# Windowed attention beside sliced projections, modulation steps two at a time, and a gapped convolution

## The chip, the cores and the metric

The kernel runs on one core of a Trainium2 chip. The metric is device time in microseconds (us) of one execution, lower is better, quoted as a median of several runs.

## The reference

The model has two layers. It carries 512 latent tokens and 256 context tokens of width 1024, 768 tokens in all. A conditioning vector makes nine modulation vectors per layer (shift, scale and gate for three sublayers) by one product with `w_mod`; context tokens have their own. Cut to what matters, for the latent tokens of a layer:

```python
m = silu(c) @ w_mod[l] + b_mod[l]                       # 9 vectors of 1024
h += 0.5 * m[2] * swiglu(modulate(rms_norm(h, g1), m[0], m[1]), ...)
z = split_in(modulate(rms_norm(h, gm), m[3], m[4]) @ w_in[l])
o_a = dense_attend(mla_q(z[0]), mla_kv(z[1], z[2]))     # 4 heads, 768 keys
o_b = b_g * dw_conv(c_g * x, w_sc)                      # 3 taps
o_c = window_attend(q, k, v, k_ctx, v_ctx, sink)        # blocks of 128, neighbours and context
o_d = silu(layer_norm(dw_conv(a * sigmoid(g), w_cf) + b))   # 31 taps
h += m[5] * concat(o_a, o_b, o_c, o_d) @ w_out[l]
h += 0.5 * m[8] * swiglu(modulate(rms_norm(h, g2), m[6], m[7]), ...)
```

In layer 0 the context tokens take the same way. In layer 1 they only give keys and values, so there 512 tokens are queries. The latent stream is normed once more at the end.

## The kernel before

Activations lie with channels on partitions and tokens along the free axis. Each large product is done in fp32r with both sides split into a high and a low part: `mm3` (L162) issues three matmuls, low by high, high by low, high by high. The split of a weight is a copy on ACT (L133) and a subtraction on VectorE (L134). Each layer runs the FFN, the mixer, the output projection (`out_proj`) and the second FFN, which in layer 1 only sees the latent tokens.

The modulation vectors are made beside all of this. `mod_group` (L179) computes four blocks of 256 columns in eight steps. A step loads 512 KB of `w_mod` on SP's queue into one of two buffers (`mraw`) and issues four matmuls of 32 rows by 256 columns into one PSUM bank (`pmod`). `fill()` takes one step; it is called after units of work in the FFNs and in the mixer, so that these steps lie between other matmuls. `need()` takes all steps that are still missing when a vector is wanted.

`mixer` runs four groups. All read one product with `w_in`, cut into 17 tiles of 128 columns, each a sum over eight blocks of 128 channels in PSUM (`proj_parts`). In the order of the program these are first the four conformer tiles (CFA, CFG); then the conformer convolution on VectorE, put at the lowest priority (`P_CONV`), so that its taps are placed behind whatever else VectorE can do; then the tiles of MLA's keys and values (KV) and queries (QA, QB), each with its sums of squares; then five of the windowed attention (WQ, WK, WV) and six of the short convolution (SC). The first MLA queries are made inside the last of these. A pool of three PSUM tiles of two banks serves the projections; the third is given back afterwards and becomes two single banks for transposes.

Then a loop runs over units. A `Latent` unit handles one head and two blocks of 128 queries of MLA against 768 keys (12 units in layer 0, 8 in layer 1). A `Window` unit handles one block of queries for the two heads that share keys (12 and 8). Each unit goes through softmax (scores on TensorE, reduce L818 or L870 on VectorE, exp on ACT, scaling on GpSimd or VectorE), `turned` (transposes L595 and splits) one step of the loop later, and `values` (L765, L766) two steps later. All latents come first, then the windows; one `fill()` stands after each step. The windows' operands are made two steps before the latents end, the conformer norm during and after the windows, and `out(i)` splits a finished block of 128 mixed channels for `out_proj`.

The program's text is not the final order of each engine: a scheduler places instructions by readiness and priority, and `rise` raises or lowers the priority of what is inside it.

The convolution takes 31 taps of one operation each per segment: latent (512) and context (256) tokens apart in layer 0, so that no tap reads across the seam.

## Time and profile before

| | us |
|---|---|
| median of 3 runs | 2715.44 (2715.19 to 2719.1) |
| the profiled execution | 2716.3 |
| its span | 2714.5 |
| TensorE busy in it | 2640.3 (97%) |
| VectorE busy | 2014.1 (74%) |
| ACT busy | 1116.9 (41%) |

The mixer of layer 0 lies between about 585 and 904 us of the span, that of layer 1 between about 2050 and 2308. The FFNs, with the modulation steps between their matmuls, fill most of the rest. A row of the timeline has the start, the length, engine, line, operation, output and inputs; neighbours of one kind are one row with their number (x6), and a bracket tells how long the engine had stood idle and for whom. PEclk is the clock granted to TensorE as a share of full speed.

### The profile page before, as it was taken

The page shows a single profiled execution, that of the slowest core. Times are in us where ns is not written, and L with a number is a line of the kernel's source. Part 1 is how long each engine was busy: PE and PEld are TensorE (multiplying, and loading weights), DVE is VectorE, ACT ScalarE, POOL GpSimd, SP SyncE. Part 2 cuts the span into 40 slices and gives each one's busy share as a digit, 9 for nine tenths or more (in the row PEclk, how much of TensorE's full clock was granted, in tenths as well). Part 3 has the DMA queues.
Part 4 walks back from the last instruction along what each step waited for, and adds up shares of the span by engine and source line. Part 5 has one row for each costly group of instructions (what it writes and reads, how often), then busy time and mean ns, then how long its engine had stood idle before and what let it go on. Part 6 is the DMA issues. An engine that isn't in the chain of part 4 may idle for free.

```text
span 2714.5 us, 40707 instructions
## 1 busy us (share of the span) xinstructions
PE 2640.3 (97%) x16021; PEld 2443.1 (90%) x16021; DVE 2014.1 (74%) x3940; ACT 1116.9 (41%) x2098; POOL 66.0 (2%) x88
## 2 busy tenths in 40 slices
PE   7999999999988999999999999999999989999998
PEld 5999999988866989999999999999998866899998
DVE  5777667679787476777667867776678786788887
ACT  4324323343376442333234523343244376544444
POOL 0000000000022000000000000000000022000000
PEclk9999999999989999999999999999999989999999
DMA  7323223321123342323223132222223223323322
GB/s 269 109 91 104 86 87 101 101 85 56 53 80 128 95 139 82 107 88 107 80 86 124 49 100 69 64 78 63 63 79 101 69 67 113 117 86 104 99 94 78
DMA packets 78271, 254.67 MB, mean 94 GB/s; under 512 B 8704, under 2 KB 14336, under 8 KB 77824
## 3 DMA queue, kind: packets, MB, share of 16 engines
q1 hardware_dynamic: 78080, 252.08, 29.2%
q8 instruction: 125, 2.05, 0.3%
q14 instruction: 66, 0.54, 0.1%
HBM read 249.95 MB, written 2.10 MB: 93 GB/s over the span
## 4 chain that ended last, share of the span: by engine, by line
PE 91%; DVE 4%; ACT 3%; DMA 1%; issue 1%; POOL 0%; DVEq 0%; SPq 0%; ACTq 0%; POOLq 0%
PE ps L162 74%; PE pone L162 8%; PE pmod L162 3%; PE pmod L179 3%; PE ps L595 1%; DMA mraw<-in_w_mod 1%; PE pone L765 1%; PE pone L766 1%; ACT f L826 1%; DMA raw<-in_w_gu 0%; ACT f L133 0%; DVE r L134 0%; ACT f L873 0%; POOL f L833 0%; PE pone L272 0%
## 5 line engine op out<-in xcount | busy, mean ns | idle before, releaser
L162 PE MATMUL ps<-x,wh 128*128 128x384 f32 (+1 forms) x3064 | 749.5, 329 | 0.0
L162 PEld LDWEIGHTS ps<-x,wh 128*128 128x128 f32 x3064 | 543.1, 188 | 0.2
L162 PE MATMUL ps<-x,wl 128*128 128x384 f32 (+1 forms) x1532 | 506.5, 331 | 0.0
L133 ACT ACTIVATE wh<-raw 128x512 fp32r<-128x512 f32 x439 | 274.8, 627 | 464.6 <-PE ps L162 313.9
L162 PE MATMUL ps<-t,wh 128*128 128x384 f32 (+2 forms) x1488 | 385.2, 341 | 0.1
L134 DVE TENSOR_TENSOR wl<-raw,wh 128x512 fp32r<-128x512 f32 x439 | 301.6, 688 | 104.9 <-ACT wh L133 102.5
L162 PE MATMUL ps<-r,wh 128*128 128x512 f32 (+3 forms) x1362 | 338.0, 350 | 0.3 <-DVE r L291 0.3
L296 DVE SCALAR_TENSOR_TENSOR h<-ps,hg,h 128x256 f32<-128x256 f32 (+3 forms) x404 | 186.9, 506 | 186.1 <-PE ps L162 185.3
L162 PEld LDWEIGHTS ps<-x,wl 128*128 128x128 f32 x1532 | 287.8, 188 | 12.9 <-issue 10.7
L162 PEld LDWEIGHTS ps<-t,wh 128*128 128x128 f32 x1488 | 269.2, 188 | 7.0 <-DVE t L134 0.4
L133 ACT ACTIVATE wh<-t 128x512 fp32r<-128x512 f32 x217 | 136.3, 630 | 335.9 <-PE ps L162 199.7
L162 PEld LDWEIGHTS ps<-r,wh 128*128 128x128 f32 (+1 forms) x1362 | 228.0, 188 | 31.8 <-DVE r L291 1.5
L450 DVE TENSOR_TENSOR t<-t,ps 128x384 f32<-128x384 f32 (+1 forms) x422 | 217.4, 521 | 51.6 <-PE ps L162 49.9
L162 PE MATMUL ps<-t,wl 128*128 128x384 f32 (+2 forms) x744 | 253.4, 342 | 1.2 <-ACT t L133 1.2
L134 DVE TENSOR_TENSOR wl<-t,wh 128x512 fp32r<-128x512 f32 x217 | 149.3, 690 | 95.2 <-ACT wh L133 94.9
L133 ACT ACTIVATE t<-t 128x384 fp32r<-128x384 f32 (+2 forms) x247 | 130.3, 537 | 213.1 <-DVE t L444 101.9
L162 PE MATMUL ps<-r,wl 128*128 128x512 f32 (+4 forms) x681 | 212.2, 352 | 1.3 <-ACT r L290 1.3
L162 PE MATMUL ps<-x,t 128*128 128x384 f32 (+1 forms) x1308 | 204.4, 310 | 0.0
L162 PEld LDWEIGHTS ps<-x,t 128*128 128x128 f32 x1308 | 194.4, 188 | 0.0
L162 PE MATMUL ps<-t,t 128*128 128x384 f32 (+2 forms) x948 | 188.8, 345 | 0.0
L162 PEld LDWEIGHTS ps<-t,t 128*128 128x128 f32 x948 | 165.4, 188 | 10.9 <-issue 1.2
L134 DVE TENSOR_TENSOR t<-t,t 128x384 fp32r<-128x384 f32 (+2 forms) x247 | 137.7, 569 | 26.0 <-ACT t L133 25.7
(229 smaller groups left out, 3774.1 us busy)
## 6 DMA issues: line engine op xcount, KB each, us to landing
raw<-in_w_gu SPq DMA_DIRECT2D x160, 512.0 KB, 3.8
mraw<-in_w_mod SPq DMA_DIRECT2D x128, 512.0 KB, 4.0
raw<-in_w_dn SPq DMA_DIRECT2D x88, 512.0 KB, 3.7
raw<-in_w_in SPq DMA_DIRECT2D x34, 512.0 KB, 3.5
raw<-in_w_out SPq DMA_DIRECT2D x20, 512.0 KB, 3.5
i<-in_w_mod SPq DMA_DIRECT2D x32, 256.0 KB, 5.9
raw<-in_w_gu SPq DMA_DIRECT2D x32, 256.0 KB, 3.5
h<-in_h SPq DMA_DIRECT2D x4, 768.0 KB, 6.8
```

The costliest lines, as they stand in the source:

```text
L133: self.nc.scalar.activation(hi, x, AF.Copy)
L134: self.nc.vector.tensor_tensor(out=lo, in0=x, in1=hi.bitcast(F32), op=ALU.subtract)
L162: self.nc.tensor.matmul(ps[:, c:e], a, b[:, c:e], start=start and i == 0, stop=stop and i == 2)
L179: nc.tensor.matmul(ps[32 * j:32 * j + 32, :256], self.sc[:, k, :], r[:, j * 256:(j + 1) * 256], start=k == 0, stop=k == KD - 1)
L296: nc.vector.scalar_tensor_tensor(out=self.h[:, k, s:e], in0=ps[:, s - a:e - a], scalar=gate[:, k, i:i + 1], in1=self.h[:, k, s:e], op0=ALU ...
L450: eng.tensor_tensor(out=out, in0=p, in1=q, op=op)
L595: self.nc.tensor.transpose(out, in_, self.ident)
L765: nc.tensor.matmul(po[:, :256], v, p[1], start=start, stop=False)
L766: nc.tensor.matmul(po[:, :256], v, p[0], start=False, stop=stop)
L826: nc.scalar.activation(pr[:, c0:], pss[g][:, c0:TOK], AF.Exp, scale=scale, bias=mx[:, g:g + 1], accum_out=sm[:, g:g + 1])
```

## The change

Order of the mixer. After the conformer tiles only WQ, WK and WV are projected. The window operands follow, and then the loop runs the window units first and the latents after them. The other nine tiles (SC, KV, QA, QB) become a generator, `others`, which yields after each of a tile's eight blocks: 72 pieces, dealt out over the three slots of each window unit. A piece accumulates its 512 columns in `pmod` and the remaining 256 in the last bank of a four-bank PSUM tile (`quad`), whose other banks hold the unit's scores for two heads. No modulation step can run in that time, since `pmod` is taken; an open group is finished first. With the first latent unit all MLA preparation comes at once: query and key weights, rotary parts, queries, keys and values. The conformer norm and the splits `out(i)` move into the latents.

Modulation. `spot()` notes that a step is due and takes both as soon as two are due; it replaces `fill()` in the FFNs and in `out_proj`. In the mixer each step of the loop over latents takes two.

Convolution. The input lies in one row with gaps of 15 zeros before, between and after the segments (written by GpSimd), so a tap is one operation over 783 elements in layer 0 and 512 in layer 1. The norm copies its result back to contiguous tiles.

Buffers. Four wide tiles come in, full tiles go from 14 to 11 and rounded ones from 27 to 26.

```diff
-    WIN, CN = 2, (2, 4, 0, 1)
+    CN = (4, 6, 8, 9)
...
+    GAP = CF_K // 2
+    WIDE = TOK + 3 * GAP
...
+    def spot(self, n=1):
+
+        self.owed += n
+        if self.owed > 1:
+            self.fill(self.owed)
+            self.owed = 0
...
-            self.fill(fills)
+            self.spot(fills)
...
+    def gap_conv(self, y, u, w, bias, n):
+
+        nc = self.nc
+        mid = CF_K // 2
+        for j in [mid] + [j for j in range(CF_K) if j != mid]:
+            if j == mid:
+                nc.vector.tensor_scalar(out=y[:, :n], in0=u[:, j:j + n], scalar1=w[:, j:j + 1], scalar2=bias, op0=ALU.mult, op1=ALU.add)
+            else:
+                nc.vector.scalar_tensor_tensor(out=y[:, :n], in0=u[:, j:j + n], scalar=w[:, j:j + 1], in1=y[:, :n], op0=ALU.mult, op1=ALU.add)
...
-        dbls = self.psum(st, 2, 1024)
-        third = st.enter_context(ExitStack())
-        self.dbl = dbls + self.psum(third, 1, 1024)
-        sgl = deque()
+
+        quad, third = self.psum(st, 1, 2048)[0], self.psum(st, 1, 1024)[0]
+        dbls = deque((quad[:, :1024], quad[:, 1024:]))
+        self.dbl = dbls + deque([third])
+        sgl = deque((third[:, :512], third[:, 512:]))
+        spare = quad[:, 1536:]
...
+        gap = self.GAP
+
+        places = [(a, b, a + i * gap) for i, (a, b) in enumerate(segs)]
         for i in range(2):
+            u = self.wide.popleft()
+            for c in [0] + [p + gap + b - a for a, b, p in places]:
+                nc.gpsimd.memset(u[:, c:c + gap], 0.0)
...
-            u = self.S()
-            nc.scalar.activation(u[:, :n], pg[:, :n], AF.Sigmoid)
-            nc.vector.tensor_tensor(out=u[:, :n], in0=pa[:, :n], in1=u[:, :n], op=ALU.mult)
+            for a, b, p in places:
+                v = u[:, p + gap:p + gap + b - a]
+                nc.scalar.activation(v, pg[:, a:b], AF.Sigmoid)
+                nc.vector.tensor_tensor(out=v, in0=pa[:, a:b], in1=v, op=ALU.mult)
...
+                for g, c, cc in ((0, w.c0[0], SEQ), (1, 1024, TOK)):
+                    q = wqs[kv][g]
...
+                    def near():
...
+                                nc.tensor.matmul(quad[:, c:c + w.n], a, b[:, kc], start=i == 0, stop=False)
...
+                    if g == 0:
+                        near()
+                    for i, (a, b) in enumerate(parts):
+                        nc.tensor.matmul(quad[:, cc:cc + CTX], a, b[:, SEQ:], start=i == 0, stop=i == 1)
+                    if g == 1:
+                        near()
+                wide = w.n + CTX
+                src = [quad[:, c:c + wide] for c in w.c0]
...
-                    ps = self.turn(dbls)
...
-                    nc.vector.reduce_max(mx[:, g:g + 1], ps[:, c0:TOK], axis=AX.X, negate=True)
-                    pss.append(ps)
+                    nc.vector.reduce_max(mx[:, g:g + 1], src[g], axis=AX.X, negate=True)
...
-        for i in range(2):
-            pc = proj(T_SC + 2 + i, n)
-            t = self.S()
...
-            px = proj(T_SC + 4 + i, n)
-            nc.vector.tensor_tensor(out=t[:, :n], in0=px[:, :n], in1=t[:, :n], op=ALU.mult)
...
-            if i == 1:
-                first_queries()
-            pb = proj(T_SC + i, n)
...
+        def slow(t, nt, m=P):
+
+            rw = self.load(win[l, t], 1024)
+            w = [self.unit(rw[:, :512]), self.unit(rw[:, 512:])]
+            pieces = [(0, SEQ, self.mod_ps)] + ([(SEQ, nt, spare)] if nt > SEQ else [])
+            for k in range(KD):
+                wh, wl = w[k // 4]
+                c = slice((k % 4) * P, (k % 4) * P + m)
+                for a, b, ps in pieces:
+                    self.mm3(ps[:m, :b - a], (wh[:, c], wl[:, c]), (x[k][0][:, a:b], x[k][1][:, a:b]), k == 0, k == KD - 1)
+                yield
+            return pieces
+
+        def others():
+
+            for i in range(2):
+                t = self.S()
+                for a, b, ps in (yield from slow(T_SC + 2 + i, n)):
+                    nc.scalar.activation(t[:, a:b], ps[:, :b - a], AF.Copy)
+                for a, b, ps in (yield from slow(T_SC + 4 + i, n)):
+                    nc.vector.tensor_tensor(out=t[:, a:b], in0=ps[:, :b - a], in1=t[:, a:b], op=ALU.mult)
...
+                self.give(t)
+                for a, b, ps in (yield from slow(T_SC + i, n)):
+                    nc.vector.tensor_tensor(out=cv[:, a:b], in0=ps[:, :b - a], in1=cv[:, a:b], op=ALU.mult)
+                ob.append(cv)
...
+            pk = yield from slow(T_KV, TOK)
+            ckv, sq = self.S(), self.S()
...
+            pq = yield from slow(T_QA, n)
...
+            pq = yield from slow(T_QB, TOK, 96)
...
+            mqb = lat["qb"] = self.R()
...
+        units = [Window(t, kv) for kv in range(2) for t in range(nq)]
+        units += [Latent(h, tp) for h in range(4) for tp in range(nq // 2)]
+        nw, per = 2 * nq, nq // 2
+        window_operands()
+        while self.open:
+            self.fill()
...
-        kw = kv_weights()
-        mla_keys(0, kw)
-        self.give(qb)
-        mla_values(kw)
-        units[0].softmax()
-        qw = query_weights()
-        out(2, ob[0])
-        out(3, ob[1])
         lt, lv = self.LAGS
-        cn = conformer_norm()
...
+        cn, rest, done, total = conformer_norm(), others(), 0, 9 * KD
...
+            nonlocal done
+            while done < min(total, round(total * share)):
+                next(rest, None)
+                done += 1
...
+            j = i - nw
+            if j == 0:
+                more(1)
+                for _ in rest:
+                    pass
+                qw, kw = query_weights(), kv_weights()
+                mla_rotary(*qw)
+                mla_queries(0, *qw)
+                mla_keys(0, kw)
+                self.give(lat["kr"])
+                mla_values(kw)
...
                     units[i].softmax()
+            if j in (nq - nw, 0):
+                self.give(*wqs[j == 0], *wks[j == 0])
...
+                if j < 0:
+                    more((3 * i + u + 1) / (3 * nw))
...
-            if i == nl - self.WIN:
-                window_operands()
-            if i - nl in self.CN[:2] or i - len(units) in self.CN[2:]:
...
+            if j in self.CN:
...
+            if j == 5:
                 out(4, oc[0])
-            self.fill()
+                out(5, oc[1])
+            if j == 6:
+                out(2, ob[0])
+                out(3, ob[1])
+            if j == nw // 2 + lv:
+                out(0, oa[0])
+            if j >= 0:
+                self.spot(2)
...
+        out(1, oa[1])
+        self.give(*vt)
...
-            self.fill()
+            self.spot()
...
-    N_R, N_F = 27, 14
+    N_R, N_F, N_WIDE = 26, 11, 4
```

What this does to TensorE's queue is seen at three places. The first is the FFN of layer 0. `ps` are its sums, `x` and `t` activations, `wl` and `wh` split weights, and `pmod<-mraw` a modulation step of four matmuls. Before:

```order
L162 MATMUL ps_394<-x_526,t_546 128x384
L162 MATMUL ps_394<-x_530,t_542 128x384
L162 MATMUL ps_394<-x_526,t_542 128x384
L179 MATMUL pmod<-mraw_66,sc 32x256 x4
L162 MATMUL ps_374<-x_486,wl_68 128x384
L162 MATMUL ps_374<-x_490,wh_67 128x384
L162 MATMUL ps_374<-x_486,wh_67 128x384
```

After:

```order
L172 MATMUL ps_394<-x_526,t_546 128x384
L172 MATMUL ps_394<-x_530,t_542 128x384
L172 MATMUL ps_394<-x_526,t_542 128x384
L189 MATMUL pmod<-mraw_65,sc 32x256 x4
L189 MATMUL pmod<-mraw_66,sc 32x256 x4
L172 MATMUL ps_374<-x_486,wl_68 128x384
L172 MATMUL ps_374<-x_490,wh_67 128x384
```

Where one step stood, two stand, and the next place, 49 rows on, has none.

The second place is a window unit of layer 0. `ident` rows are transposes, `pone` rows the values, `ps_5065` and `ps_5069` the scores of the two heads. Before:

```order
L595 MATMUL ps_6305<-ident,f_4905 128x128
L179 MATMUL pmod<-mraw_65,sc 32x256 x3
L179 MATMUL pmod<-mraw_66,sc 32x256 x4
L765 MATMUL pone<-f_4888,r_5061 128x256
L812 MATMUL ps_5065<-r_5045,r_5029 128x384
L812 MATMUL ps_5065<-r_5021,r_5029 128x384
L815 MATMUL ps_5065<-masks_r,ident_r 128x128 x2
L817 MATMUL ps_5065<-r_5045,r_5029 128x256
L817 MATMUL ps_5065<-r_5021,r_5029 128x256
```

After, `ps_5060` is the four-bank tile, and the rows with `wh` and `wl` are a piece of a projection:

```order
L172 MATMUL ps_5060<-r_5012,wl_76 128x256
L172 MATMUL ps_5060<-r_5016,wh_75 128x256
L172 MATMUL ps_5060<-r_5012,wh_75 128x256
L605 MATMUL ps_5064<-ident,f_4936 128x128
L605 MATMUL ps_5064<-ident,f_4944 128x128
L756 MATMUL pone<-f_4887,r_5052 128x256
L757 MATMUL pone<-f_4875,r_5052 128x256
```

Pieces of projections stand between a unit's transposes and values, where modulation steps stood.

The third is the preparation of MLA in layer 0. Before, with the values' weights first and the first scores last (96 channels are a head's key):

```order
L162 MATMUL ps_5065<-wl_70,r_5021 128x256
L162 MATMUL ps_5065<-wh_69,r_5021 128x256
L179 MATMUL pmod<-mraw_65,sc 32x256 x4
L179 MATMUL pmod<-mraw_66,sc 32x256
L162 MATMUL ps_5069<-r_4957,r_5053 128x512
L162 MATMUL ps_5069<-r_4957,r_5053 128x256
L162 MATMUL ps_5069<-r_4961,r_5049 128x512
```

After, the rows at L907 are the second part of the queries, from `w_uq`:

```order
L907 MATMUL ps_5060<-r_4956,wl_68 128x512
L907 MATMUL ps_5060<-r_4956,wl_68 128x256
L907 MATMUL ps_5060<-r_4956,wh_67 128x512
L907 MATMUL ps_5060<-r_4956,wh_67 128x256
L189 MATMUL pmod<-mraw_65,sc 32x256 x4
L189 MATMUL pmod<-mraw_66,sc 32x256
L172 MATMUL ps_5060<-r_5036,wl_76 128x512
L172 MATMUL ps_5060<-r_5036,wl_76 128x256
L172 MATMUL ps_5060<-r_5040,wh_75 128x512
```

The queries, which were made among the projections, stand in one piece with keys and values, and modulation steps lie among them.

## Rows read from the trace of the kernel before

**Rows 1.** Page, parts 2 and 6: the clock in 40 slices; loads of modulation weights.
```profile
PEclk9999999999989999999999999999999989999999
...
mraw<-in_w_mod SPq DMA_DIRECT2D x128, 512.0 KB, 4.0
```

**Rows 2.** Table of stretches: PE, PEld, DVE, ACT, POOL busy; PEclk, DMA share, GB/s.
```profile
585.00:745.00 160.00, 158.57 (x909) 136.22 (x907) 137.05 (x252) 57.08 (x90) 0.00 (x0) 0.99 0.20 63
745.00:757.00 12.00, 7.37 (x42) 4.85 (x40) 10.69 (x18) 7.96 (x12) 0.00 (x0) 0.72 0.38 120
757.00:829.00 72.00, 63.82 (x419) 51.53 (x417) 58.73 (x128) 53.77 (x102) 19.02 (x23) 0.91 0.27 83
829.00:904.00 75.00, 67.70 (x504) 52.92 (x503) 52.54 (x145) 48.20 (x126) 16.70 (x25) 0.98 0.35 113
...
2172.00:2188.00 16.00, 12.85 (x76) 8.81 (x74) 13.45 (x22) 11.43 (x20) 0.00 (x0) 0.82 0.58 172
2188.00:2245.00 57.00, 48.53 (x290) 40.04 (x290) 49.99 (x97) 44.04 (x78) 16.23 (x15) 0.87 0.13 38
```

**Rows 3.** Timeline of PE, in an FFN: one modulation step (start, length).
```profile
1008.14 0.69 PE L162 MATMUL ps<-x,x 128*128 128x384 f32 x3
1008.75 0.64 PE L179 MATMUL pmod<-mraw,sc 128*32 128x256 f32 x8
1009.32 0.45 PE L162 MATMUL ps<-x,wl 128*128 128x384 f32 x1
1009.61 0.51 PE L162 MATMUL ps<-x,wh 128*128 128x384 f32 x2
```

**Rows 4.** Timeline of PE, in an FFN: two modulation steps together.
```profile
1084.18 1.20 PE L162 MATMUL ps<-t,t 128*128 128x384 f32 x6
1085.31 1.07 PE L179 MATMUL pmod<-mraw,sc 128*32 128x256 f32 x16
...
1086.60 0.52 PE L162 MATMUL ps<-x,wh 128*128 128x384 f32 x2
```

**Rows 5.** Timeline of PE, window units of layer 0.
```profile
863.44 0.28 PE L765 MATMUL pone<-f,r 128*128 128x256 f32 x1
863.56 0.28 PE L766 MATMUL pone<-f,r 128*128 128x256 f32 x1
...
866.73 0.51 PE L812 MATMUL ps<-r,r 128*128 128x384 f32 x2
867.08 0.33 PE L815 MATMUL ps<-masks_r,ident_r 128*128 128x128 f32 x2
867.25 0.34 PE L765 MATMUL pone<-f,r 128*128 128x256 f32 x1
...
888.20 0.98 PE L595 MATMUL ps<-ident,f 128*128 128x128 f32 x7 [0.70 <-POOL f L833]
```

**Rows 6.** Line 818, the window units' reduces, layer 0, then layer 1.
```profile
L818 DVE TENSOR_REDUCE sm<-ps x24: 415/692/826, 829.2 to 887.0; 128x1 f32<-128x512 f32 x8, 128x1 f32<-128x640 f32 x8, 128x1 f32<-128x256 f32 x8
...
L818 DVE TENSOR_REDUCE sm<-ps x16: 677/748/826, 2245.0 to 2289.9; 128x1 f32<-128x512 f32 x8, 128x1 f32<-128x640 f32 x8
```

**Rows 7.** Timeline of ACT, projections of layer 0: the first copy out of a tile.
```profile
650.98 0.81 ACT L694 ACTIVATE f<-ps 64x768 f32<-64x768 f32 x1 [3.53 <-PE ps L162]
...
664.78 0.81 ACT L721 ACTIVATE f<-ps 128x768 f32<-128x768 f32 x1 [3.57 <-PE ps L162]
...
673.18 0.81 ACT L721 ACTIVATE f<-ps 128x768 f32<-128x768 f32 x1 [3.57 <-PE ps L162]
```

**Rows 8.** Timelines of PE, start of the MLA units: modulation steps that waited.
```profile
760.89 0.64 PE L179 MATMUL pmod<-mraw,sc 128*32 128x256 f32 x8 [1.96 <-DMA mraw<-in_w_mod]
...
2182.85 1.08 PE L179 MATMUL pmod<-mraw,sc 128*32 128x256 f32 x8 [2.30 <-DMA mraw<-in_w_mod]
```

**Rows 9.** Timeline of ACT, projections of layer 1: a table load.
```profile
2093.71 1.28 ACT L259 ACT_TABLE_LOAD   x1
2095.01 0.27 ACT L259 ACTIVATE rc<-ps,eps 128x6 f32<-128x6 f32 x1
```

**Rows 10.** Line 613, the convolution's taps, both layers.
```profile
L613 DVE SCALAR_TENSOR_TENSOR f<-f,vec,f x192: 441/737/767, 611.5 to 2171.4; 128x511 f32<-128x511 f32 x16, 128x497 f32<-128x497 f32 x8, 128x498 f32<-128x498 f32 x8, 128x499 f32<-128x499 f32 x8
```

More of the change, by code (lines that the diff above doesn't have):

```diff
@@ L457, in gate_up @@
         for m, M in enumerate(mats):
-            self.fill(fills)
+            self.spot(fills)
             for step in (1, 2, 5, 6, 7, 4, 3):
@@ L697, in mixer @@
-        nc.scalar.activation(qb[64:96, :], pqb[64:96, :TOK], AF.Copy)
-        pr = self.one
-        for t in range(nq):
-            s = slice(t * P, (t + 1) * P)
-            nc.tensor.matmul(pr[:, 2 * t:2 * t + 2], sqa[:, s], self.ones[:, :2], start=True, stop=False)
-            nc.tensor.matmul(pr[:, 2 * t:2 * t + 2], sqb[:64, s], self.ones[:64, :2], start=False, stop=True)
-        self.give(sqa, sqb)
-        rq = self.rq[l][:, :2 * nq]
-        self.rsqrt(rq, pr[:, :2 * nq], 1.0 / 192)
@@ L732, in conformer_norm @@
         def conformer_norm():
-            self.give(*us)
-            pm = self.sums(self.turn(dbls), [(y, P) for y in dd], n)
-            for y in dd:
-                nc.vector.scalar_tensor_tensor(out=y[:, :n], in0=pm[:, :n], scalar=-1.0 / 256, in1=y[:, :n], op0=ALU.mult, op1=ALU.add)
+            self.give(*(u[:, :TOK] for u in us))
+            pm = self.turn(dbls)
+            for i, y in enumerate(dd):
+                for a, b, p in places:
+                    nc.tensor.matmul(pm[:, a:b], self.ones, y[:, p:p + b - a], start=i == 0, stop=i == 1)
+            zs = [self.S(), self.S()]
+            for y, z in zip(dd, zs):
+                for a, b, p in places:
+                    nc.vector.scalar_tensor_tensor(out=z[:, a:b], in0=pm[:, a:b], scalar=-1.0 / 256, in1=y[:, p:p + b - a], op0=ALU.mult, op1=ALU.add)
+            self.give(*(y[:, :TOK] for y in dd))
             yield
             sqs = [self.S(), self.S()]
-            for y, sq in zip(dd, sqs):
-                nc.scalar.activation(sq[:, :n], y[:, :n], AF.Square)
+            for z, sq in zip(zs, sqs):
+                nc.scalar.activation(sq[:, :n], z[:, :n], AF.Square)
             yield
@@ L1037, in mixer @@
+        for i in range(len(units) + lv):
+            j = i - nw
[9 more added lines that the diff above has]
+                mla_values(kw)
+            if j == self.PAIR[per]:
                 mla_queries(2, *qw)
-                self.give(*mqa, mqb, *rot)
+                self.give(*lat["qa"], lat["qb"], *rot)
```

180 lines of the change are left out of this document (83 added, 97 removed).

## The prediction

> **What bounds the kernel now.** The profiled execution took 2716.3 us with a span of 2714.5; the median of the three timed runs is 0.9 us lower, so the sum below is made against 2716.3 and 0.9 comes off at the end. I read the page first. TensorE's granted clock is full but for the slices around the two mixers [rows 1]; the reader is to see that outside them there is nothing to win but work itself. So a gain has two sources: cheaper matmuls anywhere, or the stretches of a mixer in which TensorE waits. Next I read the table of stretches [rows 2]. The projections of layer 0 (585 to 745) hold TensorE busy 158.6 of 160 us. Then it does worse: 7.4 of 12 us while the first MLA operands are made, 63.8 of 72 in the MLA units ("latents"), 67.7 of 75 in the window units with the tail, at mean clocks of 0.72, 0.91 and 0.98 (means of stretches at 2.4 and at 1.2 GHz). Layer 1 repeats it: 12.9 of 16 at 0.82, 48.5 of 57 at 0.87. "Busy" flatters these stretches, because a short matmul's record is longer than the step to the next: the 256-column products have records of 0.28 us and follow each other every 0.12 [rows 5]. I therefore price TensorE's work by the steps between starts. Last I read the timelines of single places: a modulation step alone and two together, a window unit, the copies that end each projection tile, and the waits on modulation weights.
>
> **1. Modulation in pairs, outside the mixers.** A step is four 256-column matmuls of 32 rows each (eight records). Alone it lies between six 384-column products: from 1008.14 to 1009.61 are 1.47 us for four of those and the step [rows 3]. Within a row such products follow each other every 0.173 us (six records, 1.20 us, of which the last lasts 0.34: five steps of 0.172) [rows 4]. So the step costs 1.47 - 4 x 0.173 = 0.78. Two together: 1084.18 to 1086.60 are 2.42 us with seven products, 2.42 - 7 x 0.173 = 1.21 for two steps [rows 4]. A second step thus adds 0.43, and each interruption has a fixed price of 0.35. The order of instructions (which holds no times) counts 68 interruptions with 78 steps outside the mixers before and 40 with 68 after. That is 28 x 0.35 = 9.8 for the interruptions and 10 x 0.43 = 4.3 for steps that move into the mixers: **-14**. Their loads still run on SP's queue beside FFN work; two are asked for at once and the next pair is some 25 us away, while one lands 4.0 us after issue [rows 1].
>
> **2. Window units beside projections.** Today the units stand alone: 829.2 to 887.0 for 12 of them, 2245.0 to 2289.9 for 8 [rows 6], and their chain (reduce, exp, scaling on GpSimd, transposes, splits, values) lets TensorE wait. Their own TensorE work by steps [rows 5]: 384 columns 0.175, 256 columns 0.12, a mask 0.085, a transpose 0.117 (seven in 0.98, the last record about 0.28: 0.70 / 6). A unit of three blocks has 4, 14, 4 and 10 of these (context scores and values are the 256-column ones): 0.70 + 1.68 + 0.34 + 1.17 = 3.9. Two blocks: 16 of 256, two masks, eight transposes: 3.0. A unit that only sees the context has 8 and 4 transposes: 1.4. Layer 0 has four of each, 33 us; layer 1 four of each of the first two, 28. With nine projection tiles sliced between them (72 pieces over 36 slots in layer 0) the chain's latency has cover, and this stage becomes TensorE work. Full cover gives 58 - 33 = **-25** and 45 - 28 = **-17**; no cover gives nothing.
>
> **3. The projection stage loses its small stalls.** Tiles end every 8.4 us in layer 0 (664.78, 673.18), but the pair around the MLA query ends 13.8 apart (650.98, 664.78), an excess of 5.4 of which the sums of squares take about one [rows 7]. Spread over slots it should go: **-4**, and for layer 1, whose queries are 512 of 768 columns, two thirds of it, **-3**; the ends are 0 and 5.4 each.
>
> **4. What the new windows stage gives back.** The slices accumulate in one bank (512 columns) and a quarter of another tile (256), with no second buffer: after each tile's eighth piece the next tile waits until the copy out has ended. A copy of 768 columns lasts 0.81 on ACT [rows 7], in a queue that also holds exps, and on VectorE it stands behind a convolution tap. Nine tiles at one such wait of 0.6 to 0.7 (somewhat under that copy, since it comes in two parts) are **+6** and **+5**; it is nothing if the window units' matmuls fill it, and 12 and 10 at two waits each. The units' scores, too, lie in one tile of four banks now instead of two alternating ones of two; a unit used both before, so this is booked at nothing.
>
> **5. The latents stage becomes longer.** It takes 36 modulation steps in layer 0 instead of 11 (preamble and latents; the other 15 stood among the windows) and 24 instead of 7: at 0.43 and about 16 and 10 more interruptions at 0.35 this is 16 and 11 if all is paid, 0 if all falls into waits that the stage has anyway (72 us hold 63.8 busy). I take half, **+8** and **+5.5**. The MLA preparation, of which the first queries stood inside the projections, now stands alone between the stages, as the keys and values did in the 12 us with 7.4 busy [rows 2]: **+2** each, from 0 to the 4.6 that were idle there. The conformer norm and out-splits move in, the window operands move out; by the rows' counts on VectorE these are 9 to 10 us against 8 to 9, taken as nothing. Activation tables are loaded 7 times more (29 against 22 in the order), 1.28 each [rows 9]: 9 us of ACT, which is idle half of these stages; half of three loads per layer on the path, **+2** each.
> Here a page speaks against the change. The trace has 1.28 us for a table load. The Trainium skill, "ScalarE: Activation LUTs", section "What ACT_TABLE_LOAD costs", counts 2.66 us for a switch, load and drain together, so seven switches would be 19 us of ACT and these terms +4 instead of +2; the row shows the load alone, and the next ACTIVATE starts 0.02 after it, so this trace shows no drain behind a load.
>
> **6. The conformer convolution.** A tap over 511 elements has a median of 0.74, the shortest form (256 less an edge) 0.44 [rows 10]; per element that is 0.30 / 256 = 1.15 ns and the rest, 0.14 us, is fixed. One tap over 783 should then take 1.05 against 1.18 for two, 62 times: 8 us less of VectorE in layer 0 (about 6 by starts, since neighbours overlap), and half a us more in layer 1, where nothing joins. I book **0**: it has the lowest priority, in the projections it runs under TensorE's matmuls, and VectorE is busy 137 of 160 us there [rows 2] without keeping TensorE waiting. If that cover is gone (the windows stage now has these taps beside softmax and splits), it is worth -6. The four gap memsets per tile run on GpSimd, idle at that point.
>
> **Sum.** -14 outside the mixers; -25 - 4 + 6 + 12 = -11 in layer 0; -17 - 3 + 5 + 9.5 = -5.5 in layer 1. Together -30.5: 2716.3 - 30.5 - 0.9 = **2685**.
>
> **Rivals.**
> (a) *The latents stage swallows the mixer's gain.* Everything of step 5 is paid (23 and 16 with +5 preambles and dear tables, 25 and 20 at most, 20 above my terms) and step 4 costs two copies a tile (11 above): the sum would be near nothing; taken half way, -14 stays: **2701**. For it: TensorE's clock there is 0.72 to 0.91 already [rows 2]. Against: the latents hold 8 us of waits in layer 0 to take steps.
> (b) *Everything finds cover.* Slices cost nothing between tiles (-11) and the modulation steps fall into waits (-13.5): **2660**. For: the units leave TensorE free in between. Against: pieces come in fixed places, after a wait has begun.
> (c) *The pairs don't pay,* since the second weights have not landed where the first had: 14 us back, **2699**, with rows that show waits at L189 in the FFNs. Against: 4.0 us to landing, some 25 between pairs.
> (d) *Slower: modulation weights pace the latents.* There are two modulation buffers. A pair frees them together, both loads then run, and TensorE, in order, stands at the next pair until both are there. A pair is due every unit: 6.0 us in layer 0 (72 over 12), 7.1 in layer 1 (57 over 8) [rows 2]. Two loads of 512 KB at the 172 GB/s of the stretch 2172 to 2188 are 6.1 us [rows 2]. Where steps came close together, TensorE waited 1.96 and 2.30 us for a load [rows 8]. With about 30 pairs in both mixers, at 2.3 each: +69, **2754**. It decides from an average of 30.5 / 30 = 1.0 us a pair; slower by more than 0.2% from 1.2. Against: one load lands in 4.0 [rows 1], and little else moves in that stage, so a pair should be there in under 6.
>
> **How the numbers follow.** My forecast 58%; (a) 14%, (b) 12%, (c) 3%, (d) 13%. Against its own bounds the forecast's terms reach from 2664 to 2704. The range takes in (a), (c) and half of (b): 2660 to 2708; out are (d) and the edges. 0.2%, about what a measurement of this kernel can tell from no change, is 5.4 us. Faster by more: the forecast, (b), (c) and most of (a), 0.82; within 0.2%: 0.06, from (a) at its dear end and (d) at half its price; slower 0.12.
>
> **What would show it.** Right: the FFN stretches shorter by 14 us in sum at clock 1.00; window reduces spread over some 110 us in layer 0 (nine tiles at 8.4 and 33) with TensorE's steps close to back to back; the latents stretch near 85 us. Wrong: rows of TensorE waiting at the modulation matmuls for loads of a us or more in every unit (d); waits of slices for copies at each ninth piece, above one us (step 4); a VectorE without gaps in the windows stage, with taps ahead of what TensorE waits for, which would move the end of that stage and give the convolution's 6 us their worth; a clock under 0.9 through the latents (a).

## The result and the profile after

The changed kernel took 2815.7 us (2813.6 to 2818.8, 4 runs) against 2717.3 for the kernel before: a ratio of 1.036, 95% interval 1.034 to 1.038. It is slower by about 98 us; the prediction was 2685, faster, with a range to 2708. The profiled execution had a span of 2813.5. Below, a measured total without a ratio is that of a single run.

Two lines of the page of the changed kernel, from parts 1 and 2 (busy time by engine, the clock in 40 slices):

```profile
PE 2671.9 (95%) x16021; PEld 2462.4 (88%) x16021; DVE 2010.0 (71%) x3882; ACT 1127.1 (40%) x2113; POOL 72.1 (3%) x98
...
PEclk9999999999968899999999999999999979999999
```

Against [rows 1], the clock has its low places in slices 12 to 14 and 33, the mixers, as low as 0.6. The FFNs are not the place. From the last accumulation of one FFN into `h` to the first of the output projection, the mixers take 395.7 and 304.5 us (326.5 and 262.0 before). The first FFN takes 3.4 us less, all that lies between the mixers 10.7 less, and the tail 1.4 more: -3.4 + 69.2 - 10.7 + 42.5 + 1.4 = +99.0, which is the difference of the spans.

The table of stretches of the changed kernel, with the columns of [rows 2]. In layer 0: first projections, windows with the slices, last slices, MLA preparation, latents; then the same five in layer 1:

```profile
585.00:664.00 79.00, 75.32 (x416) 62.86 (x415) 72.73 (x109) 32.06 (x51) 0.00 (x0) 1.00 0.25 81
664.00:782.00 118.00, 108.86 (x675) 94.24 (x676) 93.90 (x190) 56.02 (x137) 21.40 (x23) 0.97 0.12 38
782.00:798.00 16.00, 15.24 (x81) 12.12 (x80) 7.47 (x14) 8.22 (x14) 0.83 (x2) 0.76 0.20 54
798.00:827.00 29.00, 17.49 (x96) 10.36 (x94) 14.89 (x26) 14.24 (x22) 0.00 (x0) 0.68 0.44 134
827.00:960.00 133.00, 101.08 (x600) 69.22 (x601) 63.81 (x142) 60.00 (x110) 17.91 (x23) 0.80 0.34 107
...
2107.00:2176.00 69.00, 65.97 (x322) 53.13 (x322) 62.20 (x106) 31.13 (x51) 0.00 (x0) 0.98 0.24 81
2176.00:2258.00 82.00, 73.41 (x412) 61.74 (x412) 67.22 (x135) 38.47 (x87) 13.79 (x14) 0.98 0.14 42
2258.00:2276.00 18.00, 16.58 (x112) 13.19 (x111) 9.91 (x21) 12.94 (x27) 1.37 (x2) 1.00 0.22 68
2276.00:2305.00 29.00, 17.80 (x91) 10.53 (x91) 14.52 (x26) 12.21 (x22) 0.00 (x0) 0.72 0.47 154
2305.00:2392.00 87.00, 63.52 (x405) 44.88 (x405) 47.70 (x100) 41.88 (x76) 14.15 (x15) 0.88 0.29 91
```

Read against [rows 2]: projections and windows of layer 0 together are 79 + 118 + 16 = 213 us, where they were 160 and 58. The preparation is 29 (12 before), and the latents are 133, at a mean clock of 0.80, where they were 72 at 0.91. In layer 1 it is, from the end of the FFN, 170 against 166, 29 against 16, and 87 against 57. So nearly the whole loss lies in the MLA units, whose code the change hardly touches: their units have the same matmuls, reduces and exps, and what came in beside them are modulation steps, the conformer norm and splits. Their reduces, first and last start, layer 0 and layer 1:

```profile
L871 DVE TENSOR_REDUCE sm<-ps x24: 424/957/958, 827.3 to 957.8; 128x1 f32<-128x768 f32 x16, 128x1 f32<-128x256 f32 x8
...
L871 DVE TENSOR_REDUCE sm<-ps x16: 948/958/959, 2304.9 to 2389.9; 128x1 f32<-128x768 f32 x16
```

Before, the same 24 reduces went from 756.6 to 828.9.

What TensorE waited for in the latents of layer 0 (total, times, longest):

```profile
PE ps L172 <- ACT f L874: 10.5, 7, 3.7
PE pmod L189 <- DMA mraw<-in_w_mod: 9.5, 11, 2.1
PE ps L605 <- DVE f L144: 7.3, 7, 1.5
```

Three candidates stand there: an exp (L874) ahead of scores, loads of modulation weights, and splits (L144) ahead of transposes. The chain of waits from 779 to 960 us names the second most (its first line, the shares by line):

```profile
by line: DMA mraw<-in_w_mod 22.2%; PE ps L172 20.6%; PE pmod L189 11.8%; PE ps L605 7.4%; ACT f L874 3.1%; PE pone L756 3.0%; DVE sm L871 2.9%; DVE r L144 2.8%; PE pone L757 2.6%; PE ps L282 2.6%; ACT r L143 2.5%; PE pmod L172 2.3%; issue 2
```

22.2% of 181 us are 40. Pieces of it (start, length, what):

```profile
862.61 0.60 PE pmod L189 x6
...
863.22 3.75 DMA mraw<-in_w_mod
...
867.01 0.68 PE pmod L189 x8
...
867.72 3.99 DMA mraw<-in_w_mod
...
871.75 0.40 PE pmod L189
```

A step ends, 3.75 us pass until the next buffer has landed, a step, 3.99 us, a step. This is what rival (d) described, in the place and with the sign that it gave.

### The profile page after: what moved, and what is told of

It reads as the page before. It is cut to its first block, busy times and chain, and to the rows that moved or that the text cites. A ratio compares the mean times of both kernels' runs of the same rounds, so it can differ in the third digit from the quotient of the medians.

```text
span 2813.5 us, 40621 instructions
## 1 busy us (share of the span) xinstructions
PE 2671.9 (95%) x16021; PEld 2462.4 (88%) x16021; DVE 2010.0 (71%) x3882; ACT 1127.1 (40%) x2113; POOL 72.1 (3%) x98
## 4 chain that ended last, share of the span: by engine, by line
PE 64%; DVE 5%; DMA 4%; ACT 3%; issue 1%; POOL 0%; DVEq 0%; ACTq 0%; POOLq 0%
PE ps L172 47%; PE pmod L172 5%; PE pone L172 5%; DMA mraw<-in_w_mod 3%; PE pmod L189 2%; PE ps L605 1%; DVE f L630 1%; DMA raw<-in_w_gu 1%; DVE f L144 1%; DVE wl L144 1%; PE pone L756 0%; PE pone L757 0%; ACT f L143 0%; DVE r L144 0%; DVE sm L871 0%
## 5 line engine op out<-in xcount | busy, mean ns | idle before, releaser
L172 PE MATMUL ps<-x,wh 128*128 128x384 f32 (+1 forms) x3064 | 748.7, 329 | 0.0
L172 PEld LDWEIGHTS ps<-x,wh 128*128 128x128 f32 x3064 | 542.4, 188 | 1.5 <-issue 1.2
L172 PE MATMUL ps<-x,wl 128*128 128x384 f32 (+1 forms) x1532 | 504.7, 330 | 0.5 <-ACT x L300 0.5
L172 PE MATMUL ps<-t,wh 128*128 128x384 f32 (+2 forms) x1488 | 385.4, 341 | 0.3 <-DVE t L144 0.3
L144 DVE TENSOR_TENSOR wl<-raw,wh 128x512 fp32r<-128x512 f32 x437 | 301.1, 690 | 103.2 <-ACT wh L143 100.9
L172 PEld LDWEIGHTS ps<-x,wl 128*128 128x128 f32 x1532 | 287.5, 188 | 7.4 <-issue 3.3
L172 PEld LDWEIGHTS ps<-t,wh 128*128 128x128 f32 x1488 | 269.2, 188 | 7.2 <-DVE t L144 0.5
L172 PE MATMUL ps<-r,wh 128*128 128x512 f32 (+3 forms) x1074 | 261.5, 339 | 2.8 <-DVE r L301 2.8
L172 PE MATMUL ps<-t,wl 128*128 128x384 f32 (+2 forms) x744 | 253.1, 341 | 1.1 <-ACT t L143 1.1
L144 DVE TENSOR_TENSOR wl<-t,wh 128x512 fp32r<-128x512 f32 x217 | 149.1, 689 | 90.3 <-ACT wh L143 90.3
L172 PE MATMUL ps<-x,t 128*128 128x384 f32 (+1 forms) x1308 | 204.2, 309 | 0.0
L172 PEld LDWEIGHTS ps<-r,wh 128*128 128x128 f32 (+1 forms) x1074 | 182.0, 190 | 22.8 <-DVE r L301 4.2
L172 PEld LDWEIGHTS ps<-x,t 128*128 128x128 f32 x1308 | 194.1, 188 | 0.0
L172 PE MATMUL ps<-t,t 128*128 128x384 f32 (+2 forms) x948 | 189.0, 346 | 0.0
L172 PE MATMUL ps<-r,wl 128*128 128x256 f32 (+3 forms) x537 | 173.2, 345 | 8.7 <-ACT r L300 3.5
L172 PEld LDWEIGHTS ps<-t,t 128*128 128x128 f32 x948 | 165.7, 188 | 10.1 <-issue 0.4
L144 DVE TENSOR_TENSOR t<-t,t 128x384 fp32r<-128x384 f32 (+2 forms) x247 | 137.5, 568 | 25.0 <-ACT t L143 24.6
```

What stands on the lines that cost most here:

```text
L144: self.nc.vector.tensor_tensor(out=lo, in0=x, in1=hi.bitcast(F32), op=ALU.subtract)
L172: self.nc.tensor.matmul(ps[:, c:e], a, b[:, c:e], start=start and i == 0, stop=stop and i == 2)
```

## Experiments: are the modulation steps the cause?

Theory P took the chain at its word: the weights of the steps pace the latents. Theory C said that MLA's own chain is long and the steps only fall into its waits. Three kernels tell them apart, and a fourth does the pairs alone.

**Steps moved out of the mixers.**

```diff
-    FILLS = (1, 1, 0, 0)
+    FILLS = (2, 2, 0, 0)
...
-            if j >= 0:
-                self.spot(2)
...
-            self.spot()
+            self.spot(2)
```

> The changed kernel with no modulation step in the mixer: the 60 steps of the two latents stages are taken in the FFNs and the output projection of layer 0 instead, always two at a time. Theory P (weights of the steps pace the latents: a step put into TensorE's queue early stands there until its 512 KB have landed, with two buffers, and everything behind it waits): the latents shrink from 133 to about 80 us and from 87 to about 62, the preparation ahead of them from 29 to about 22 each, while the FFNs take 60 more steps at 0.43 to 0.55, +26 to +33: 2815 - 92 + 30 = about 2753. Theory C (what makes these stages long is MLA's own chain, which no projection covers any more; the steps only fall into its waits): the stages lose little, the FFNs still pay 30: 2815 to 2845.

Measured: 2846.1 us, ratio to before 1.048 (1.046 to 1.050), a us above what Theory C gave. The FFNs pay as expected (607.1 to the end of the first against 583.1, 1136.5 between the mixers against 1127.2), and the mixers take 396.0 and 304.3 us, where they had 395.7 and 304.5. By TensorE's rows 46 of the 60 steps, with 23 MB of loads, have left the mixers: all of layer 1's, and in layer 0 all but eight in the preparation and six from 965 us on. Neither mixer got shorter. The latents of layer 0 in this kernel, and what TensorE waited for in them:

```profile
852.00:985.00 133.00, 92.95 (x419) 73.32 (x422) 62.83 (x135) 59.27 (x107) 17.90 (x24) 0.68 0.07 20
```

```profile
PE ps L172 <- ACT f L874: 17.4, 8, 4.1
PE ps L605 <- DVE f L144: 11.2, 9, 2.5
```

They last 133 us again (their reduces go from 851.9 to 982.5). The waits for loads are gone, and the other two have grown: scores stand 17.4 us for exps instead of 10.5, transposes 11.2 for splits instead of 7.3. TensorE does less in this stage, and its mean clock is 0.68 instead of 0.80, a mean of its two levels, 1.2 and 2.4 GHz, nearer to the lower.

**Steps without loads.**

```diff
...
-                nc.sync.dma_start(r[:, o:o + w], self.a["w_mod"][l, k * P:(k + 1) * P, c:c + w])
+                if not self.dry:
+                    nc.sync.dma_start(r[:, o:o + w], self.a["w_mod"][l, k * P:(k + 1) * P, c:c + w])
...
             if j >= 0:
+                self.dry = True
                 self.spot(2)
+                self.dry = False
```

> The changed kernel, but the modulation steps of the latents load no weights: they multiply what the buffer last held, so these modulation vectors are not computed. The matmuls and their places stay. Theory P: the waits for loads on the chain (40 us from 779 to 960 in layer 0, and as many in layer 1 as its share says, some 30) and the half clock behind them go: about 2735 to 2750. Theory C: the waits are taken over by MLA's chain: 2800 to 2815.

Measured: 2806.0 us, with mixers of 395.1 and 300.0, as Theory C had it. Of 128 loads 78 are left; those still cost TensorE 3.6 us in the latents of layer 0, against 9.5.

**Four buffers for the steps.**

```diff
+                lent = [self.raw.popleft() for _ in range(2)]
+                self.mraw.extend(lent)
                 qw, kw = query_weights(), kv_weights()
...
```

> The changed kernel with four instead of two buffers for modulation weights in the preparation and the latents (two of the four buffers for other weights are lent). Theory P, if the latency of a load is what counts: a step has twice the time, half to all of the 70 us of waits go: 2745 to 2780. If the rate of the loads counts, it gains little, since the clumps of steps are only longer: 2795 to 2815. Theory C: 2810 to 2820.

Measured: 2804.0 us, mixers 388.2 and 299.3. This run alone decides nothing: it lies 6 below what Theory C gave and in the range of Theory P for the case that the rate of the loads counts. But with the two before it Theory P has fallen: the 40 us of loads on the chain of layer 0 were worth 0 to 8 us there. Behind these waits others stood, as the rows of the first of these three kernels show.

**The pairs alone, on the kernel before.**

```diff
-            self.fill(fills)
+            self.spot(fills)
```

> The kernel before, with steps taken two at a time in the FFNs and the output projection, and nothing else. By the terms of the prediction 28 interruptions less at 0.35 are -9.8 (2707); by the price read in the changed kernel's trace (0.23 for each pair joined) -6.5 (2711). The mixers should not change.

Measured: 2701.8 us, ratio 0.995 (0.994 to 0.997), so 13 us less, more than either expectation. The mixers took 325.1 and 260.4. By the starts of TensorE's rows outside the mixers the steps cost 54 us there instead of 62, 8 less for 24 joins; where the rest of the 13 sits, the rows don't show. Pairs pay, at least what was forecast.

## Experiments: the PSUM tiles

If the steps were not it, the other two waits remained: scores behind an exp, transposes behind a split. Two stretches show the order of one unit's two query blocks. Before, scores (L162), reduce (L870), scores of the next block, exp (L873) of the first:

```profile
800.02 1.33 PE L162 MATMUL ps<-r,r 96*128 96x512 f32 x6
...
801.39 0.96 DVE L870 TENSOR_REDUCE sm<-ps 128x1 f32<-128x768 f32 x1 [0.21 <-PE ps L162]
...
801.81 1.30 PE L162 MATMUL ps<-r,r 96*128 96x512 f32 x6
...
803.60 0.99 ACT L873 ACTIVATE f<-ps,sm,rq 128x768 f32<-128x768 f32 x1 [1.35 <-DVE sm L871]
```

In the changed kernel, scores (L172), reduce (L871), exp (L874), and only then the next scores:

```profile
899.30 1.32 PE L172 MATMUL ps<-r,r 96*128 96x512 f32 x6
...
900.65 0.96 DVE L871 TENSOR_REDUCE sm<-ps 128x1 f32<-128x768 f32 x1 [1.04 <-PE ps L172]
...
902.96 0.99 ACT L874 ACTIVATE f<-ps,sm,rq 128x768 f32<-128x768 f32 x1
...
904.10 2.29 PE L172 MATMUL ps<-r,r 96*128 96x512 f32 x6 [2.90 <-ACT f L874]
```

Before, the second scores start 1.79 us after the first, and as much ahead of the first's exp. After, they start 4.80 us later, 0.06 behind the end of the exp and the read of its sum, and TensorE stood 2.90 us for it. The second scores don't need that exp: they go to the other half of the ring. But that half is no longer a tile of its own. Before, `dbls` were two tiles of two banks and `sgl` two of one bank. Now they are halves of `quad` and of `third`. The names in the order ahead of the prediction had it: `ps_5065` and `ps_5069` before, `ps_5060` alone after.

Theory T: work for one half of a tile is ordered behind the readers of the other half. Theory U: the chain is that long wherever nothing covers it.

**Tiles apart in the latents.**

```diff
-        quad, third = self.psum(st, 1, 2048)[0], self.psum(st, 1, 1024)[0]
+        early = st.enter_context(ExitStack())
+        quad, third = self.psum(early, 1, 2048)[0], self.psum(early, 1, 1024)[0]
...
+                early.close()
+                dbls.clear(), sgl.clear()
+                dbls.extend(self.psum(st, 2, 1024)), sgl.extend(self.psum(st, 2, 512))
                 qw, kw = query_weights(), kv_weights()
```

> The changed kernel, but before the MLA preparation the four-bank and the two-bank PSUM tile are given back and taken again as two tiles of two banks and two of one bank, as the kernel before had them for these units. Theory T (the two halves of one tile are ordered as one: the scores of the next block wait until exp has read the block before, and a transpose waits for the split of the other half): the latents go from 133 to about 80 us and from 87 to about 62, the preparations lose 5 each, the clock there rises: 2815 - 53 - 25 - 10 = about 2727. Theory U (MLA's chain is that long wherever nothing covers it): 2800 to 2815.

Measured: 2725.1 us, ratio to before 1.003 (1.002 to 1.005): 91 us back with a few lines that move no work in the program's text (about ten modulation steps now run after the mixers). Windows, preparation and latents of layer 0:

```profile
664.00:780.00 116.00, 107.84 (x670) 93.74 (x671) 92.09 (x188) 56.99 (x139) 22.18 (x24) 0.97 0.12 38
795.00:811.00 16.00, 11.26 (x75) 7.40 (x74) 12.52 (x22) 13.25 (x22) 0.00 (x0) 0.89 0.42 129
811.00:893.00 82.00, 70.98 (x503) 53.62 (x502) 59.90 (x136) 60.21 (x109) 18.61 (x23) 0.94 0.41 129
```

The latents are 82 us at a mean clock of 0.94, the preparation is 16.

**Tiles apart in the windows stage too.**

```diff
-        quad, third = self.psum(st, 1, 2048)[0], self.psum(st, 1, 1024)[0]
...
+        early, mid = st.enter_context(ExitStack()), st.enter_context(ExitStack())
+        self.dbl = self.psum(early, 3, 1024)
+        dbls, sgl = deque(list(self.dbl)[:2]), deque()
...
+        early.close()
+        sgl.extend(self.psum(st, 2, 512))
+        quad, spare = self.psum(mid, 1, 1536)[0], self.psum(mid, 1, 512)[0]
...
+                mid.close()
+                dbls.clear()
+                dbls.extend(self.psum(st, 2, 1024))
```

The projections ahead of the windows have three tiles of two banks again, too.

> As the run before, and in the windows stage too the single tiles are apart: three banks for a unit's scores, one bank for the slices' 256 columns, two single banks for transposes. Theory T: the slices no longer wait for exps and the transposes not for each other's splits; of the some 20 and 16 us that the windows stages of both layers lie above the 110 and 84 of their TensorE work half goes: about 18 below the run before. Theory U: as the changed kernel, 2800 to 2815.

Measured: 2698.9 us, ratio 0.994 (0.992 to 0.996), 26 below the run before, where 18 was expected. The five stretches of each layer:

```profile
582.00:664.00 82.00, 80.53 (x469) 68.84 (x459) 79.09 (x122) 37.43 (x62) 0.00 (x0) 1.00 0.27 90
664.00:768.00 104.00, 100.45 (x646) 88.80 (x646) 87.62 (x184) 52.83 (x132) 22.56 (x24) 1.00 0.12 34
768.00:782.00 14.00, 13.80 (x85) 11.18 (x84) 7.01 (x13) 8.23 (x13) 0.00 (x0) 0.88 0.30 102
782.00:797.00 15.00, 10.08 (x77) 6.43 (x76) 12.26 (x21) 11.92 (x18) 0.00 (x0) 0.89 0.56 175
797.00:881.00 84.00, 74.79 (x491) 56.28 (x490) 59.32 (x134) 61.08 (x109) 18.64 (x23) 0.87 0.38 116
...
2039.00:2101.00 62.00, 61.05 (x306) 50.81 (x307) 58.07 (x99) 29.64 (x49) 0.00 (x0) 0.97 0.28 92
2101.00:2174.00 73.00, 68.27 (x401) 58.47 (x400) 69.51 (x137) 37.26 (x86) 13.62 (x14) 1.00 0.15 46
2174.00:2191.00 17.00, 16.81 (x93) 13.63 (x93) 7.63 (x16) 9.91 (x22) 1.66 (x2) 1.00 0.21 63
2191.00:2213.00 22.00, 17.77 (x111) 12.41 (x109) 16.40 (x30) 16.20 (x28) 0.00 (x0) 0.84 0.35 104
2213.00:2267.00 54.00, 49.80 (x343) 36.73 (x343) 46.58 (x95) 38.56 (x74) 16.01 (x15) 1.00 0.34 109
```

The windows with their slices take 104 us instead of 116 to 118 in layer 0, and 73 instead of 82 in layer 1, both at a clock of 1.00. The mixers as a whole take 326.0 and 251.4 us (326.5 and 262.0 before the change).

**The kernel before with halves.** The reverse: the kernel before, with its latents and windows on halves.

```diff
...
         third.close()
-        sgl.extend(self.psum(st, 2, 512))
+        first.close()
+        quad, two = self.psum(st, 1, 2048)[0], self.psum(st, 1, 1024)[0]
+        dbls.clear()
+        dbls.extend((quad[:, :1024], quad[:, 1024:]))
+        sgl.extend((two[:, :512], two[:, 512:]))
```

> The kernel before, but its PSUM for latents and windows is cut the way the changed kernel has it: two halves of one four-bank tile for scores, two halves of one two-bank tile for transposes. Nothing else changes. Theory T (halves of one tile are ordered as one): latents +50 and +25, and the windows, which there take a half for each head, +10 to +20 in both layers together: 2790 to 2830. Theory U: 2713 to 2719.

Measured: 2842.4 us, 124 more than before, from this edit alone; even the expectation was short. The mixers take 396.9 and 318.4 us, as long as those of the changed kernel or longer. The latents of layer 0, the reduces of its windows, and what TensorE waited for from 740 to 960 us:

```profile
763.00:881.00 118.00, 86.33 (x452) 65.09 (x450) 62.96 (x136) 56.63 (x107) 18.65 (x24) 0.75 0.20 61
```

```profile
L819 DVE TENSOR_REDUCE sm<-ps x24: 397/692/826, 882.1 to 956.9; 128x1 f32<-128x512 f32 x8, 128x1 f32<-128x640 f32 x8, 128x1 f32<-128x256 f32 x8
```

```profile
PE ps L595 <- DVE f L134: 16.7, 16, 3.0
PE pmod L179 <- DMA mraw<-in_w_mod: 9.2, 10, 1.8
PE ps L162 <- ACT f L874: 7.3, 6, 2.9
```

The latents are 118 us (72 before), and the windows' reduces take 75 (58 before [rows 6]). Transposes wait for splits and scores for exps, as in the changed kernel. This kernel, too, gives its tiles back and takes new ones, so it isn't the giving back that helped. With this run and the two before it the cause is shown, both ways: tiles cut into halves cost the time, the same banks as tiles of their own don't. Which part of building the program orders one half behind the other, no run shows. The Trainium skill, "PSUM — Partial Sum Buffer", section "PSUM bank collisions raise a hardware error", keeps two engines from the same bank at the same time and lets different banks be; the halves here are whole banks, so its rule asks for no such wait, and the same banks taken as tiles of their own ran without it.

## Experiments: what was left

**Most taps left out** (30 of 31 in each convolution):

```diff
-        for j in [mid] + [j for j in range(CF_K) if j != mid]:
+        for j in [mid]:
```

> The changed kernel with one of the 31 taps of the conformer convolution, so 120 operations on VectorE are left out. If taps on VectorE end the windows stages (they are 10.7% and 9.3% of the chain there, 20 us), 2795 to 2800; if they lie under other waits, 2808 to 2815.

Measured: 2801.5 us, between the two; the mixer of layer 0 lost 10.3 us, that of layer 1 0.4. On halves, taps held something in layer 0. It was not tried with the tiles apart.

**The convolution alone, on the kernel before.**

```diff
...
+                y = self.wide.popleft()
+                a, b, p = places[-1]
+                self.gap_conv(y, us[i], self.vcol(l, "wcf", i * CF_K, CF_K), self.vcol(l, "bcf", i), p + b - a)
...
```

> The kernel before with the gapped convolution alone (four wide tiles for four full ones). By the prediction VectorE loses some 6 us beside TensorE's work in the projections and nothing ends earlier: 2713 to 2717; if VectorE had held something there, 2709 to 2711; if the norm's copy or the gaps cost, up to 2720.

Measured: 2716.2 us, ratio 1.0003 (0.9994 to 1.0012): nothing.

With the tiles apart, three kernels asked again what the steps in the latents cost.

**Without loads,** the edit as above:

```diff
...
             if j >= 0:
+                self.dry = True
                 self.spot(2)
+                self.dry = False
```

> The changed kernel with all PSUM tiles apart (2699 us), and the modulation steps of the latents load no weights, so these vectors are not computed. What the loads still cost there is what goes: TensorE's waits for them have 4.0 and 0.5 us in the two latents stretches, and the preparations some more: 2690 to 2696. If they are paid by something else: 2697 to 2701.

Measured: 2687.2 us, 12 below, more than was expected. The mixer of layer 0 went from 326.0 to 317.0, that of layer 1 from 251.4 to 251.9.

**Without steps,** again as above:

```diff
+    FILLS = (2, 2, 0, 0)
...
-            if j >= 0:
-                self.spot(2)
...
-            self.spot()
+            self.spot(2)
```

> The changed kernel with all PSUM tiles apart and no modulation step in the mixers; the FFNs of layer 0 take the 60 steps in pairs, +33 by the earlier run (FFN stretches 607.1 against 583.1 and 1136.5 against 1127.2). If the steps in the latents are now paid in full, as TensorE's share there says (0.91 of layer 0's stretch), the mixers lose 60 x 0.43 = 26 and the waits for loads, 5 to 9: about 2699. If a half was hidden: 2712. If they cost more than that there, through pieces of a chain that they delay: 2685 to 2692.

Measured: 2721.9 us, ratio to before 1.001 (1.000 to 1.002), above all three expectations. In the profiled execution, 5 us over the median, the FFNs have +37 (609.6 and 1139.9 against 582.0 and 1130.3) and the mixers -3 (319.4 and 254.7 against 326.0 and 251.4). By TensorE's rows 42 steps have left the mixers; the rest ran outside them already, or still stands in the preparation of layer 0. Between the first and the last reduce of the latents, where less than one step is left, pass 81.5 and 53.4 us instead of 82.9 and 51.8. So even here the latents take their steps almost for nothing; that what layer 0 does pay are the waits for loads is argued from the run before, not shown.

**With four buffers:**

```diff
+                lent = [self.raw.popleft() for _ in range(2)]
+                self.mraw.extend(lent)
                 qw, kw = query_weights(), kv_weights()
...
```

> The changed kernel with all PSUM tiles apart, and four buffers for modulation weights from the MLA preparation on, as in the earlier run with four. There it gave 11 us, where stalls gave each load time; here the waits for loads are 4 to 9 us in all: 2692 to 2697. If the two buffers lent are missed by the other weights: 2700 to 2705.

Measured: 2689.2 us, ratio to before 0.990 (0.988 to 0.991). That is better than was expected, and the best complete kernel of the study, 28 us below the kernel before: the whole change, with its PSUM tiles apart and two buffers lent.

## Why the prediction was wrong

**Where it failed.** Two steps. Step 4 saw that scores lie "in one tile of four banks now instead of two alternating ones of two", and booked it at nothing because a unit uses both anyway. Capacity was the wrong question; who is ordered behind whom was the right one. The term booked at nothing measured about 117 us: that is what the tiles taken apart give back (2815.7 to 2698.9), for scores and transposes together. Step 5 then took the latents of before, 72 us, as its base and added modulation steps, though it is the same tile that MLA's scores, keys, values and queries use in turn. With the tiles apart the forecast of step 5 is near: +15 us for preparation and latents of layer 0 (12 + 72 before, 15 + 84 with the tiles apart) where +12 was forecast, +3 in layer 1 (16 + 57, and 22 + 54) where it was +9.5; but ten of the 60 steps run behind the mixers there. With halves it was +78 and +43.

**Step 1** holds in the changed kernel: 14.1 us less in the FFN and output projection stretches, against 14. The close match is partly luck: in the other kernels with these pairs, the two with steps moved out of the mixers aside, the same stretches are 8 to 18 us shorter than before. A pair looks as in [rows 4]:

```profile
1209.01 0.52 PE L172 MATMUL ps<-x,wh 128*128 128x384 f32 x2
1209.46 1.07 PE L189 MATMUL pmod<-mraw,sc 128*32 128x256 f32 x16
1210.46 0.44 PE L172 MATMUL pone<-x,wl 128*128 128x384 f32 x1
```

Over all such places, from the start of the product ahead to the second product behind, less two products at 0.173, a single step costs 0.77 and a pair 1.20 (medians): joining saves 0.35 and a second step adds 0.43, as the sum had it. The 68 places before add up to 62 us, the 40 of the changed kernel to 45.

**Steps 2 and 3** were right as mechanisms, once the tiles are apart. In layer 0 the projections, windows and last slices take 82 + 104 + 14 = 200 us against 216.5 before (58 and, from the end of the FFN, 158.5), so -17 (forecast with step 4: -23); in layer 1, counted the same way, 153 against 166, -13 (forecast: -15). The windows' own matmuls, priced by steps [rows 5], fill the stage together with the slices at full clock (TensorE busy 100.5 of 104 us).

**Step 4's other half**, single banks between tiles, was too small in layer 0 by the 6 us that are missing there, if the cover of the windows is complete as the clock of 1.00 suggests; no run measured these copies alone.

**Step 5, tables.** The order's 29 loads are there, each 1.28, and the exp behind one starts 0.01 later. What they cost on the path no run shows:

```profile
828.51 1.28 ACT L874
829.80 1.09 ACT f L874 x2
```

The Trainium skill, "ScalarE: Activation LUTs", section "What ACT_TABLE_LOAD costs", counts about 1.38 us of drain with a load; this trace shows none: the exp above starts 0.01 us behind the load, and ACT starts 28 of the 29 loads within 0.04 us of its instruction before.

**Step 6** was right on the kernel before: nothing, measured by itself. (The gaps are three memsets a tile in layer 0 and two in layer 1, not four.) In the changed kernel the gaps were not measured alone; there 120 taps left out were worth 10 us in layer 0, so the price of 6 that the step kept for a lost cover is not ruled out.

**The rivals.** (d) forecast the sign, the place and, with 2754, 37 of the 98 us, and its rows are in the trace. That was luck: with 46 of the 60 steps gone the mixers took as long. With the tiles apart loads cost something, 12 us in the one run that leaves 50 of them out, 9 of these in layer 0's mixer. (a) named the stage and the fallen clock, but as a sum of dear terms. No rival asked whether two halves may be worked on at once. The terms' own ends, added up, reach from some 2650 to 2767 (an estimate from the prediction's own bounds), further than the 2664 to 2704 that it gave them, and even so not to 2815.7.

**The total.** With its tiles apart the change gives 18 us against 30.5 forecast. The mixer of layer 0, booked at -11, takes 326.0 us where it took 326.5; that of layer 1, booked at -5.5, loses 10.6. And pairs alone, on the kernel before, gave 13 of the 18: what the new order earns beside them, once its tiles are apart, is some 4 us, and the intervals of the two ratios overlap. Four buffers make it 28, but they were not tried with pairs alone, so they don't speak for the order. Single stretches of unchanged code scatter by some 3 to 5 us between runs (the tail from 401 to 406), so terms under that are not settled here.

## What to carry to other kernels

When buffers are merged or cut in another way, ask first which instructions the program now orders behind each other, not whether the bytes still fit: in the order of instructions, one tile's name where there were two is the sign. A chain of waits tells which wait ended last, not what it is worth; two waits that end close together hide each other, and only a kernel without one of them says which to mend. Try the cheap part of a change by itself: here the pairs alone gave most of what the whole could. Take the duration of a stage as a base only if everything that set it is still there.

## What the runs showed of the hardware

The length of the latents on halves did not go with the clock granted to TensorE: the stage of layer 0 took 133, 134 and 133 us at mean clocks of 0.80 (28 modulation steps in it), 0.74 (the same steps, most of their loads left out) and 0.68 (six steps). With the tiles apart it ran at 0.87 to 0.94. In the rows of the changed kernel a block's scores took 2.29 us behind a wait of 2.90 (granted clock 0.50 from 904 to 907 us, 1.2 GHz), and 1.32 without one (1.00 from 899 to 901, 2.4 GHz). Where such scores are on the chain, a wait is thus paid twice; how much of the latents that is, no run separates. Work that falls into the waits is close to free: with the tiles apart, moving 42 steps out of the mixers took 3 us from these and put 37 on the FFNs.
